# Output projection of layer 0: two early units loaded by GpSimd's queue, last column chunk split in all units

## The chip, the cores and the metric

The kernel runs on one core of one Trainium2 chip. The metric is the device time of one execution in microseconds (us), as the median of several runs. Before the change it is 2216.42 us (three runs, 2216.26 to 2216.97). "Faster" and "slower" are meant against that number.

Five engines matter here: TensorE (PE, matmuls; its weight loads are listed apart as PEld), VectorE (DVE), ScalarE (ACT), GpSimd (POOL) and SyncE (SP, which here only issues transfers). Each engine, and each queue of transfers, takes its instructions in a fixed order.

## What is computed

Two layers of a streaming encoder on 256 positions of width 2048, all in fp32. Cut to what the change touches, the reference is:

```python
for l in range(DEPTH):
    ...
    proj = h @ w_in[l]
    ...
    y_c = short_conv_mixer(sb, sc, sh, sconv_w[l])
    y_d = conformer_conv(ag, conf_w_dw[l], conf_b_dw[l], conf_ln_g[l], conf_ln_b[l])
    y = jnp.concatenate([y_a, y_b, y_c, y_d], axis=-1) @ w_out[l]
    x = layer_norm(ALPHA * x + (1.0 + gate_m) * y, post_mix_g[l], post_mix_b[l])
    h = layer_norm(x) * (1.0 + scale_f) + shift_f
    y = conv_ffn(h, ffn_w_up[l], ffn_w_conv[l], ffn_b_conv[l], ffn_w_down[l])
    ...
```

The change touches the product with `w_out` in layer 0: 2048 inputs (16 k tiles of 128, four each from the mixers a, b, c and d) by 2048 outputs, for two position tiles of 128.

## The kernel before

A weight tile goes through TensorE in one of two ways. **Exact**: the fp32 tile is used as it was loaded (tile name `wexact`), one fp32 matmul for each product; the profile counts such a matmul as two instructions. **Split**: the raw tile (`wraw`) is cast on ScalarE to a short format (`whi` or `thi`, L344), the rest is formed on VectorE by a subtraction (`wlo` or `tlo`, L345), the activation is split in the same way (`a`, L363 and L364), and three short-format matmuls stand for one product: high by high, high by low, low by high.

`out_proj` (L574) runs over three column chunks: columns 0 to 1023 in eight units of two k tiles, columns 1024 to 1535 in four units of four k tiles, and columns 1536 to 2047 in four units of four k tiles. I call them the first, second and last chunk. With `plain=(1024,)` in layer 0, the second chunk is exact, and so are the first `PLAIN_UNITS` = 2 units of the other two chunks; `exact` in `load_unit` (L703) says so. In layer 1 `plain` is empty, and all is split. The pairs `a` that were split once are kept for later chunks (`kept`).

The matmuls of the last chunk stand together at the end (`done`): position tile 0 through all four units, then position tile 1. After position tile 0, `finish` (L601) and `norm(0)` run on VectorE, then the normed rows are transposed on TensorE (`ps_xT`, L557), and the next product `first` (L501, the first columns of the feed-forward part) begins.

`weights` (L314) makes the tiles and issues their transfers. Exact tiles take buffers of the tags `whi` and `wlo` (four each) in turn, or "slot" buffers where `spare` is set (units 0 and 1 of the last chunk); raw tiles take one of four buffers, shared with the modulation weights `wmod` (1 MB each, multiplied and summed on VectorE at L193, the "mod step") and with the rows `gb` of the norm (L614). All these transfers stand in SP's queue, in the order in which the code makes them, so a transfer that waits for a buffer holds all that stand behind it. How many mod steps come between the units is set by `RATES`; a scheduler then orders each engine's instructions by its own estimates, and that order is fixed when the kernel is built. GpSimd does only small power operations and memsets.

## Time and profile before

| what | us |
|---|---|
| median of three runs | 2216.42 |
| the profiled execution, as timed | 2215.87 |
| its span, first to last instruction | 2214.1 |
| exact products of the first chunk, start on TensorE | 296.93 |
| second chunk, start on TensorE | 346.55 |
| last chunk, start on TensorE | 374.02 |
| transposes ahead of the feed-forward part, start | 402.03 |

The profile is one execution. Its times count from the first instruction; a row gives start, duration, engine, line, operation, output<-input and a count, and in brackets how long the engine had idled ahead of it and what ended that.

### The profile page before, as it was taken

The page shows a single profiled execution, that of the slowest core. Times are in us where ns is not written, and L with a number is a line of the kernel's source. Part 1 is how long each engine was busy: PE and PEld are TensorE (multiplying, and loading weights), DVE is VectorE, ACT ScalarE, POOL GpSimd, SP SyncE. Part 2 cuts the span into 40 slices and gives each one's busy share as a digit, 9 for nine tenths or more (in the row PEclk, how much of TensorE's full clock was granted, in tenths as well). Part 3 has the DMA queues.
Part 4 walks back from the last instruction along what each step waited for, and adds up shares of the span by engine and source line. Part 5 has one row for each costly group of instructions (what it writes and reads, how often), then busy time and mean ns, then how long its engine had stood idle before and what let it go on. Part 6 is the DMA issues. An engine that isn't in the chain of part 4 may idle for free. (4 is left out here: it accounts for less than half of the span.)

```text
span 2214.1 us, 28391 instructions
## 1 busy us (share of the span) xinstructions
PE 2182.7 (99%) x10868; PEld 1795.1 (81%) x10868; DVE 1705.3 (77%) x2269; ACT 1081.6 (49%) x1656; POOL 22.4 (1%) x38
## 2 busy tenths in 40 slices
PE   8999999999999999999999999999999999999997
PEld 6776865588888888888867988868888888888886
DVE  5657997798888888989958988877765656575776
ACT  3132731655454545545665555465444545464553
POOL 0000000000000000000000000000000000000000
PEclk9999999999999999999999999999999999999999
DMA  9999989598888889989757546856765555555553
GB/s 392 417 376 390 358 326 394 205 341 325 327 317 318 330 319 325 331 331 345 278 218 291 188 160 253 329 196 248 262 213 190 190 190 190 190 209 192 191 196 144
DMA packets 94442, 608.15 MB, mean 275 GB/s; under 512 B 10657, under 2 KB 10849, under 8 KB 28769
## 3 DMA queue, kind: packets, MB, share of 16 engines
q1 hardware_dynamic: 94178, 606.31, 74.3%
q8 instruction: 85, 1.39, 0.2%
q14 instruction: 51, 0.42, 0.0%
q10 hardware_dynamic: 128, 0.03, 0.0%
HBM read 604.17 MB, written 2.13 MB: 274 GB/s over the span
## 5 line engine op out<-in xcount | busy, mean ns | idle before, releaser
L344 ACT CAST whi<-wraw 128x1024 fp32r<-128x1024 f32 (+1 forms) x612 | 637.3, 1046 | 722.3 <-PE g_c L117 212.2
L345 DVE TENSOR_TENSOR wlo<-wraw,whi 128x1024 fp32r<-128x1024 f32 (+1 forms) x612 | 733.8, 1212 | 291.7 <-ACT whi L344 275.9
L193 DVE SCALAR_TENSOR_TENSOR wmod<-wmod,crep 128x2048 f32<-128x2048 f32 x192 | 438.1, 2286 | 71.7 <-DMA wmod<-in_w_mod_dram 70.8
L117 PE MATMUL v_c<-hT,whi 128*128 128x512 f32 x1408 | 489.2, 392 | 0.0
L117 PE MATMUL g_c<-hT,whi 128*128 128x512 f32 x1280 | 444.6, 392 | 0.0
L117 PE MATMUL v_c<-hT,wlo 128*128 128x256 f32 x1408 | 392.1, 279 | 0.0
L117 PE MATMUL d<-whi,a 128*128 128x512 f32 x1344 | 386.4, 389 | 0.0
L117 PE MATMUL g_c<-hT,wlo 128*128 128x256 f32 x1280 | 356.5, 278 | 0.0
L117 PEld LDWEIGHTS v_c<-hT,whi 128*128 128x128 f32 x1408 | 263.6, 187 | 59.3
L117 PEld LDWEIGHTS d<-whi,a 128*128 128x128 f32 x1344 | 252.0, 188 | 52.4
L117 PEld LDWEIGHTS g_c<-hT,whi 128*128 128x128 f32 x1280 | 239.7, 187 | 54.2
L117 PEld LDWEIGHTS v_c<-hT,wlo 128*128 128x128 f32 x1408 | 265.1, 188 | 0.1
L117 PEld LDWEIGHTS g_c<-hT,wlo 128*128 128x128 f32 x1280 | 241.0, 188 | 0.0
L117 PE MATMUL d<-wlo,a 128*128 128x512 f32 x672 | 232.9, 389 | 0.0
L117 PEld LDWEIGHTS d<-wlo,a 128*128 128x128 f32 x672 | 126.1, 188 | 26.2
L117 PE MATMUL o<-whi,a 128*128 128x512 f32 x352 | 102.1, 393 | 0.0
L363 ACT CAST a<-g 128x512 fp32r<-128x512 f32 x132 | 81.1, 615 | 17.0 <-PE d L117 15.7
L364 DVE TENSOR_TENSOR a<-g,a 128x512 fp32r<-128x512 f32 x132 | 88.7, 684 | 0.0
L501 PE MATMUL first<-wexact,hN 128*128 128x512 f32 x192 | 86.0, 598 | 1.2 <-ACT hN L120 1.0
L117 PEld LDWEIGHTS o<-whi,a 128*128 128x128 f32 x352 | 65.9, 188 | 14.9 <-issue 1.0
L1415 DVE SCALAR_TENSOR_TENSOR u<-g,par,u 128x254 f32<-128x254 f32 (+1 forms) x176 | 73.7, 476 | 0.0
L501 PEld LDWEIGHTS first<-wexact,hN 128*128 128x128 f32 x192 | 35.6, 192 | 41.2 <-issue 34.9
(311 smaller groups left out, 2161.9 us busy)
## 6 DMA issues: line engine op xcount, KB each, us to landing
wmod<-in_w_mod_dram SPq DMA_DIRECT2D x192, 1024.0 KB, 6.9
wraw<-in_ffn_w_up_dram SPq DMA_DIRECT2D x168, 1024.0 KB, 5.2
wraw<-in_ffn_w_down_dram SPq DMA_DIRECT2D x88, 1024.0 KB, 5.0
wexact<-in_w_in_dram SPq DMA_DIRECT2D x64, 512.0 KB, 11.4
wraw<-in_w_out_dram SPq DMA_DIRECT2D x24, 1024.0 KB, 5.8
wraw<-in_w_in_dram SPq DMA_DIRECT2D x24, 1024.0 KB, 5.2
wexact<-in_w_out_dram SPq DMA_DIRECT2D x16, 512.0 KB, 11.4
wexact<-in_ffn_w_up_dram SPq DMA_DIRECT2D x16, 512.0 KB, 5.7
```

The costliest lines, as they stand in the source:

```text
L117: pe.matmul(o, lhsT, rhs, start=start, stop=stop, skip_group_check=True)
L193: i = dve.scalar_tensor_tensor(out=raw, in0=raw, scalar=1.0, in1=crep, op0=ALU.mult, op1=ALU.mult, accum_out=col)
L344: held(act.copy(hi[:, :m], r), "cast")
L345: i = dve.tensor_tensor(out=lo[:, :m], in0=r, in1=hi[:, :m].bitcast(F32), op=ALU.subtract)
L363: act.copy(hi, src)
L364: dve.tensor_tensor(out=lo, in0=src, in1=hi.bitcast(F32), op=ALU.subtract)
L501: i = pe.matmul(ps, hN[kt // 4][:, kt % 4, t * P : (t + 1) * P], parts[kt], start=kt == 0, stop=kt == KT - 1, skip_group_check=True,)
L1415: dve.scalar_tensor_tensor(out=u[:, sh:], in0=x[:, : S - sh], scalar=col(k, j), in1=u[:, sh:], op0=ALU.mult, op1=ALU.add)
```

## The change

```diff
-    def weights(w, k0, nk, c0, width, exact=False, spare=0):
+    def weights(w, k0, nk, c0, width, exact=False, spare=0, queue=nc.sync):
...
-                nc.sync.dma_start(out=r[:, :m], in_=w.take(m, rows_of(l, k0 + k, per, c0, width)))
+                queue.dma_start(out=r[:, :m], in_=w.take(m, rows_of(l, k0 + k, per, c0, width)))
...
-                exact = c0 in plain or (bool(plain) and u < PLAIN_UNITS)
-                parts = weights(w, kt, nk, c0, width, exact, spare)
+                early = c0 == 0 and bool(plain) and u < PLAIN_UNITS
+                exact = c0 in plain or early
+                parts = weights(w, kt, nk, c0, width, exact, spare, nc.gpsimd if early else nc.sync)
```

It holds two edits. Units 0 and 1 of the first chunk stay exact, but their four transfers of 512 KB are issued by GpSimd. Units 0 and 1 of the last chunk are split now: four exact tiles become two raw tiles, four casts and four subtractions, and the k tiles 0 to 3, exact in the first chunk, need their activation pairs (`a<-ya`) split as well. Nothing changes in layer 1, nor in any engine's order behind layer 0's `first` products.

Three places show how the order moves. **SP's queue** at the start of the output projection; each row is a transfer, `x2` two alike. Before:

```order
L328 DMA wexact<-in_w_in_dram 128x1024 x2
L192 DMA wmod<-in_w_mod_dram 128x2048 x5
L328 DMA wexact<-in_w_out_dram 128x1024 x2
L192 DMA wmod<-in_w_mod_dram 128x2048
L328 DMA wexact<-in_w_out_dram 128x1024 x2
L192 DMA wmod<-in_w_mod_dram 128x2048
L333 DMA wraw<-in_w_out_dram 128x2048
```

And with the change, in SP's queue:

```order
L328 DMA wexact<-in_w_in_dram 128x1024 x2
L192 DMA wmod<-in_w_mod_dram 128x2048 x7
L333 DMA wraw<-in_w_out_dram 128x2048
L192 DMA wmod<-in_w_mod_dram 128x2048
L333 DMA wraw<-in_w_out_dram 128x2048
```

The four `wexact<-in_w_out_dram` are gone from it. They stand on GpSimd instead, behind the memsets of the attention part and ahead of the power operation of mixer d's norm:

```order
L1064 MEMSET rope 64x256
L1065 MEMSET rope 64x256
L328 DMA wexact<-in_w_out_dram 128x1024 x4
L147 TENSOR_TENSOR rd<-rd,mhalf 128x2
```

**VectorE in the first chunk**: `convD` and `rd`, `dgD` belong to mixer d's norm, each `wlo` row is one split unit (2 to 7, in order), and the rows begin behind the last product of `yc`. Before:

```order
L874 SCALAR_TENSOR_TENSOR convD<-ps_mean,convD 128x256 x4
L193 SCALAR_TENSOR_TENSOR wmod,sums_4_1598<-wmod,crep 128x2048
L364 TENSOR_TENSOR a<-yc,a 128x2x256 x2
L193 SCALAR_TENSOR_TENSOR wmod,sums_4_1598<-wmod,crep 128x2048
L345 TENSOR_TENSOR wlo<-wraw,whi 128x1024 x2
...
L364 TENSOR_TENSOR a<-yd,a 128x2x256
L345 TENSOR_TENSOR wlo<-wraw,whi 128x1024 x2
L193 SCALAR_TENSOR_TENSOR wmod,sums_4_1598<-wmod,crep 128x2048
L364 TENSOR_TENSOR a<-yd,a 128x2x256
L345 TENSOR_TENSOR wlo<-wraw,whi 128x1024 x2
L193 SCALAR_TENSOR_TENSOR wmod,sums_4_1598<-wmod,crep 128x2048
L345 TENSOR_TENSOR wlo<-wraw,whi 128x1024 x2
```

With the change:

```order
L193 SCALAR_TENSOR_TENSOR wmod,sums_4_1598<-wmod,crep 128x2048 x2
L875 SCALAR_TENSOR_TENSOR convD<-ps_mean,convD 128x256 x4
L345 TENSOR_TENSOR wlo<-wraw,whi 128x1024 x2
L193 SCALAR_TENSOR_TENSOR wmod,sums_4_1598<-wmod,crep 128x2048
L894 TENSOR_SCALAR rd<-ps_var 128x2
L364 TENSOR_TENSOR a<-yc,a 128x2x256
L900 TENSOR_SCALAR dgD<-cst,rd 128x128 x2
L364 TENSOR_TENSOR a<-yc,a 128x2x256
...
L364 TENSOR_TENSOR a<-yd,a 128x2x256
L364 TENSOR_TENSOR a<-ya,a 128x2x256 x2
L345 TENSOR_TENSOR wlo<-wraw,whi 128x1024 x2
L193 SCALAR_TENSOR_TENSOR wmod,sums_4_1598<-wmod,crep 128x2048
L345 TENSOR_TENSOR wlo<-wraw,whi 128x1024 x2
```

The splits `a<-yc` go behind unit 2's subtractions, one of them between `rd` and `dgD`; the two new splits `a<-ya` stand ahead of unit 6's subtractions. The number of mod steps between the units is the same.

**VectorE around the end of the second chunk**: `o_102400` and `o_102410` are the second chunk's results for position tiles 0 and 1, `o_153600` the last chunk's for tile 0. Before:

```order
L604 TENSOR_TENSOR yg<-o_102400_1969,gate_2_1368 128x512
L605 SCALAR_TENSOR_TENSOR x_96<-x_96,yg 128x512
L193 SCALAR_TENSOR_TENSOR wmod,sums_4_1598<-wmod,crep 128x2048
L608 BN_STATS st_o_1602<-x_96 128x6
L604 TENSOR_TENSOR yg<-o_102410_1970,gate_2_1368 128x512
L193 SCALAR_TENSOR_TENSOR wmod,sums_4_1598<-wmod,crep 128x2048
L605 SCALAR_TENSOR_TENSOR x_97<-x_97,yg 128x512
L223 TENSOR_TENSOR mod_4_2026<-sums_4_1598,par 128x16
L608 BN_STATS st_o_1603<-x_97 128x6
L345 TENSOR_TENSOR wlo<-wraw,whi 128x1024 x4
L604 TENSOR_TENSOR yg<-o_153600_2052,gate_2_1368 128x512
```

With the change, the same stretch:

```order
L193 SCALAR_TENSOR_TENSOR wmod,sums_4_1598<-wmod,crep 128x2048
L605 SCALAR_TENSOR_TENSOR x_97<-x_97,yg 128x512
L223 TENSOR_TENSOR mod_4_2026<-sums_4_1598,par 128x16
L608 BN_STATS st_o_1603<-x_97 128x6
L345 TENSOR_TENSOR tlo<-wraw,thi 128x1024 x4
L345 TENSOR_TENSOR wlo<-wraw,whi 128x1024 x4
L604 TENSOR_TENSOR yg<-o_153600_2070,gate_2_1368 128x512
```

The four new subtractions `tlo` (units 0 and 1) stand behind the second chunk's last statistics and ahead of units 2 and 3. On TensorE, position tile 0 of the last chunk is 48 short-format matmuls now, and three of position tile 1 stand among them, one ahead of the first `tlo` product and two near the end; 45 of position tile 1 follow.

## The prediction

> **What bounds the kernel now.** I read the page's busy times first, then the stretches around the change, the waits of TensorE, the last link of the chain of waits, and the timelines of TensorE, VectorE, ScalarE and SyncE between 260 and 440 us.

> ```profile
> span 2214.1 us, 28391 instructions
> PE 2182.7 (99%) x10868; PEld 1795.1 (81%) x10868; DVE 1705.3 (77%) x2269; ACT 1081.6 (49%) x1656; POOL 22.4 (1%) x38
> ...
> 436.00:960.00 524.00, 524.00 (x2947) 455.37 (x2948) 462.35 (x565) 272.38 (x383) 0.00 (x0) 1.00 0.89 326
> 295.00:335.00 40.00, 38.00 (x144) 25.58 (x145) 38.50 (x53) 16.79 (x22) 0.70 (x1) 1.00 0.99 377
> ...
> PE ps_xT L557 <- ACT xn L120: 3.7, 3, 3.1
> PE o L117 <- DMA wexact<-in_w_out_dram: 2.9, 1, 2.9
> ...
> 1962.76 239.42 PE d L117 x1056
> ```

> TensorE is busy for 99% of the span, and from 436 to 960 us for 524.00 of 524. What layer 0's output projection gains or loses before 436 therefore reaches the end undiminished. Two waits stand inside the changed stretch: 2.9 us for the exact weights and 3.1 us for the normed rows. But from 295 to 335 us VectorE is busy for 38.50 of 40 (third figure after the comma), as closely as TensorE's 38.00. A short-format matmul takes 239.42 / 1056 = 0.2267 us.

> **First edit: the four loads on GpSimd.** The rows are TensorE's, SyncE's and VectorE's timelines, and one line of the exact tile's answer.

> ```profile
> 268.13 7.07 PE L117 MATMUL C_c<-hF,wexact 128*128 128x256 f32 x32
> 296.93 14.00 PE L117 MATMUL o<-wexact,ya 128*128 128x512 f32 x32 [2.88 <-DMA wexact<-in_w_out_dram]
> 346.55 7.03 PE L117 MATMUL o<-wexact,ya 128*128 128x512 f32 x16
> ...
> 290.94 0.86 SPq L328 DMA_DIRECT2D wexact<-in_w_out_dram  x2
> ...
> 308.43 1.28 DVE L364 TENSOR_TENSOR a<-yc,a 128x512 fp32r<-128x512 f32 x2
> 311.85 2.35 DVE L345 TENSOR_TENSOR wlo<-wraw,whi 128x1024 fp32r<-128x1024 f32 x2
> 317.36 0.48 DVE L899 TENSOR_SCALAR dgD<-cst,rd 128x128 f32<-128x128 f32 x2 [0.88 <-POOL rd L147]
> 339.95 2.36 DVE L345 TENSOR_TENSOR wlo<-wraw,whi 128x1024 fp32r<-128x1024 f32 x2 [0.95 <-ACT whi L344]
> ```

> SyncE issues the first two loads at 290.94, behind modulation weights, and TensorE starts on them at 296.93 after 2.88 us idle. On GpSimd's queue they wait only for buffers that the C group's products (from 268.13 on) give back, about 268 us for the first and 275 for the second by the products' order. So the 2.88 us go, and the exact products start near 294.05 (296.93 - 2.88).

> That gain stops at the next stage. The order in VectorE's queue has the same subtractions and mod steps. Unit 2's first `wlo` ends at 311.85 + 1.18 = 313.02; with the two `a<-yc` (1.28 less overlap, 1.21 net) behind it, at 311.8. From there on, one `a<-yc` fills the 0.88 gap ahead of `dgD`, the two new `a<-ya` add about 1.2, and the 0.95 gap ahead of unit 7 takes some back: unit 6 comes about 0.6 later than before, unit 7 about 0.4 earlier. TensorE, busy 38.00 of 40 with 1.93 of its idle time (up to 296.93) ahead of the first product, has no slack to make up for a late unit, and a unit that isn't ready can't start early. The chunk's end at 346.55 moves by -0.4 to +0.6; I take **0**. Should VectorE not bind, the bound on this side is -2.9.

> The operation that no row shows is a large load on GpSimd's queue. From below it costs nothing (the loads land 20 us ahead of need). [...]

> ```profile
> 287.59 0.69 DVE L364 TENSOR_TENSOR a<-yb,a 128x512 fp32r<-128x512 f32 x1 [0.89 <-ACT a L363]
> ...
> DMA to landing us min/median/max: 2.9/9.5/14.9
> ```

> [...] I take **0**, nearest to the median landing of 9.5 after 275, and keep +4.7. [...]

> The second chunk stays exact and keeps its 27.47 us (346.55 to 374.02).

> **Second edit: the tail.** First the rows of TensorE, then VectorE, with layer 1's, where all is split, among them; then the loads; then one group each of subtractions and casts.

> ```profile
> 374.02 3.60 PE L117 MATMUL o<-wexact,ya 128*128 128x512 f32 x8
> 402.03 1.97 PE L557 MATMUL ps_xT<-cst,xn 128*128 128x128 f32 x8 [3.14 <-ACT xn L120]
> 435.42 0.47 PE L117 MATMUL v_c<-hT,whi 128*128 128x512 f32 x1
> 1463.66 1.36 PE L557 MATMUL ps_xT<-cst,xn 128*128 128x128 f32 x8 [0.24 <-ACT xn L120]
> 1495.80 0.48 PE L117 MATMUL v_c<-hT,whi 128*128 128x512 f32 x1
> ...
> 372.12 2.29 DVE L193 SCALAR_TENSOR_TENSOR wmod<-wmod,crep 128x2048 f32<-128x2048 f32 x1
> 375.53 2.28 DVE L193 SCALAR_TENSOR_TENSOR wmod<-wmod,crep 128x2048 f32<-128x2048 f32 x1
> 378.45 0.69 DVE L608 BATCH_NORM_STATS2 st_o<-x 128x6 f32<-128x512 f32 x1
> 390.96 0.69 DVE L604 TENSOR_TENSOR yg<-o,gate 128x512 f32<-128x512 f32 x1 [5.95 <-PE o L117]
> 391.57 0.15 DVE L629 TENSOR_REDUCE offs_o<-offs_o 128x1 f32<-128x4 f32 x1
> 1452.58 0.69 DVE L604 TENSOR_TENSOR yg<-o,gate 128x512 f32<-128x512 f32 x1 [4.30 <-PE o L117]
> ...
> 363.72 2.29 DVE L193 SCALAR_TENSOR_TENSOR wmod<-wmod,crep 128x2048 f32<-128x2048 f32 x1 [0.19 <-DMA wmod<-in_w_mod_dram]
> 365.04 1.60 SPq L333 DMA_DIRECT2D wraw<-in_w_out_dram  x2
> 377.84 0.33 SPq L614 DMA_DIRECT2D gb<-in_post_mix_b_dram  x1
> ...
> 378.92 1.99 ACT L344 CAST whi<-wraw 128x1024 fp32r<-128x1024 f32 x2 [38.05 <-DMA wraw<-in_w_out_dram]
> 386.52 0.63 ACT L622 ACTIVATE junk<-gb 128x512 f32<-128x512 f32 x1 [2.96 <-DMA gb<-in_post_mix_b_dram]
> ...
> L345 DVE TENSOR_TENSOR tlo<-wraw,thi 128x1024 fp32r<-128x1024 f32 x12 | 14.2, 1219 | 0.0
> L344 ACT CAST thi<-wraw 128x1024 fp32r<-128x1024 f32 x12 | 12.1, 1050 | 3.4 <-DMA wraw<-in_ffn_w_down_dram 1.8 <-DMA wraw<-in_w_out_dram 1.6
> ```

> Now the exact products of the tail start at once, at 374.02; position tile 0 ends with `yg` at 390.96, and the transposes follow 402.03 - 390.96 = 11.07 later. That chain stays (layer 1: 1463.66 - 1452.58 = 11.08). TensorE idles 3.14 ahead of it, because too little of position tile 1 was left.

> With the change, position tile 0's 8 exact products (7.03 for 16 instructions at 346.55) become 24 short matmuls (5.4), so TensorE has less to do; but VectorE now stands ahead of it. In its order the first `tlo` comes behind the second chunk's last statistics: 378.45 + 0.69, about 379.1. It takes 1.22, so the first low products start at 380.3. Meanwhile the two raw tiles take the buffers of earlier mod steps (the later one, at 363.72, is through at 366.0), land by 375.5 (the median of 9.5), and their casts (1.05 each) are done by 377.6: earlier than VectorE. What was started at 374.02 now waits about 5 us on VectorE. Then 49 matmuls (48, and one of position tile 1 among them) x 0.2267 = 11.1 end at 391.4, and the transposes come at 402.5: **+0.5**. Position tile 1's 45 matmuls (10.2) fill until 401.6, so TensorE idles 0.9 there instead of 3.14.

> That idle time has a price after it. From the transposes to `v_c` layer 0 takes 435.42 - 402.03 = 33.39, layer 1, with 0.24 idle ahead, 1495.80 - 1463.66 = 32.14.

> ```profile
> 296.00:298.00 2.00, 1.07 (x3) 0.59 (x4) 2.00 (x5) 0.00 (x0) 0.00 (x0) 1.00 1.07 442
> 402.00:403.00 1.00, 0.97 (x5) 0.97 (x6) 0.00 (x0) 0.68 (x1) 0.00 (x0) 0.50 0.93 393
> 405.00:406.00 1.00, 1.00 (x3) 0.43 (x3) 0.93 (x4) 1.00 (x5) 0.03 (x1) 0.99 0.00 0
> ```

> The granted clock (third from the right) is 0.50 at 402 and back at 0.99 at 405; after the 2.88 us ahead of 296.93 it stayed 1.00. With 0.9 idle I take layer 1's time: 32.14 - 33.39 = **-1.25**. But the wait at 375 to 380 is longer than 3.14, so the low clock should show there: some 3 us at half rate (402 to 405) are 1.5 us of matmuls lost, **+1.5**; its bounds are 0 and 1.8. [...]

> `gb` is pushed behind the raw tiles: it takes the buffers that the `tlo` subtractions free, until about 383.9, against 377.84 now. It landed 8.7 later (386.52); that would be 392.6, and with the four `junk` steps (2.5) behind it 395.1. VectorE's `offs_o`, which needs them, stands right behind `yg` (391.57, then 392.0): at worst +3.1. I take 0, since two transfers fewer stand ahead of it, so that it may land some 4 us sooner. The 4 casts lie in ScalarE's 38.05 idle, and cost nothing.

> Sum: 0 + 0.5 - 1.25 + 1.5 = **+0.75**. The profiled execution was timed at 0.55 under the median; I put the difference on the median: 2216.42 + 0.75 = **2217.2**.

> **Rivals.** *A: both gains arrive.* VectorE doesn't bind in either place, and the exact products' 2.88 goes through. The tail starts at 371.14, takes 11.1 + 11.07, and 32.14 to `v_c`: 425.45 instead of 435.42, -9.97, **2206.5**. Against it: VectorE's 38.50 of 40. *B: only the tail's gain.* The `tlo` would be ready at 374.02: 374.02 + 22.17 + 32.14 = 428.33, -7.1, **2209.3**. For it: layer 1's tail runs like that. Against it: the two mod steps at 372.12 and 375.53 and the statistics at 378.45 stand ahead in VectorE's fixed order. *C: slower.* The last raw tile is issued only when the mod step at 375.53 gives its buffer back, at 377.84 (now 365.04 and just behind). It decides from a landing of 8.5 on: its first `wlo` is due at 380.3 + 36 x 0.2267 = 388.5, and a cast and a subtraction (1.0 and 1.18) earlier is 386.3. With 14.9 it lands at 392.7, its `wlo` is there at 394.9, 6.4 late: +7.2, **2223.6**. For it: the raw tiles of now took 378.92 - 365.04 = 13.9. Against it: two transfers of 1 MB fewer stand ahead. *D: GpSimd's loads late*, +4.7: 0.75 + 4.7, **2221.9**. That the first edit brings no load earlier at all changes the sum by nothing.

> **How the numbers follow.** My forecast has 0.78, A 0.03, B 0.08, C 0.07, D 0.04. The forecast's own bounds are -2.9 (first edit) and -1.5 (clock) below, and +0.6 (unit 6), +0.3 (clock) and +3.1 (`gb`) above: from 2212.8 to 2221.2. The unknown price of GpSimd's loads takes the upper end to D, 2221.9, which is my range. A measurement of this kernel can tell about 0.2%, 4.4 us, from no change: faster (A, B) 0.11, same 0.78, slower (C, D) 0.11.

> **What would show it.** Right: no wait of `o` for `wexact`, but one of about 2 us for `wlo` before the same 346.5; then a wait of about 5 us on `tlo` from 375 on, with a granted clock of 0.50 behind it; the transposes near 402.5 to 404 with under 1.5 idle, and `v_c` about 32.1 after them. Wrong: a first chunk that ends 2 us or more earlier (VectorE didn't bind), `tlo` ready before 377, a wait for `wraw` in the last two units, or exact products that start after 297.

## The result, and the profile after

The changed kernel takes 2220.38 us as the median of 12 runs (2217.82 to 2227.84), the kernel before 2216.55 of 12 (2214.31 to 2218.11): a ratio of 1.002, 95% interval 1.0011 to 1.0029, so 2.4 to 6.4 us slower. A second set gave 2219.92 against 2216.64, ratio 1.0016 (1.0007 to 1.0025). The median lies inside the predicted range, and the change is smaller than the 4.4 us (0.2%) that the forecast took as no change. But it is 3.2 us above the predicted 2217.2, and where the forecast said +0.75 it is +3.3 to +3.8.

The profiled execution of the changed kernel was timed at 2217.82, the fastest of its 12. Its page and its waits of TensorE:

```profile
span 2216.0 us, 28439 instructions
PE 2182.0 (98%) x10884; PEld 1800.8 (81%) x10884; DVE 1710.6 (77%) x2275; ACT 1086.1 (49%) x1662; POOL 25.0 (1%) x42
...
PE o L117 <- DVE tlo L345: 5.7, 1, 5.7
...
PE ps_var L117 <- ACT sqD L881: 2.3, 1, 2.3
...
PE ps_xT L557 <- ACT xn L120: 1.5, 3, 1.0
```

The wait for `wexact` is gone, and the 3.1 us ahead of the transposes are 1.0. In their place stand 5.7 us for `tlo`, which was forecast, and 2.3 us for `sqD`, the squares of mixer d's norm, which was not. TensorE's timeline has these places in order:

```profile
292.19 7.03 PE L117 MATMUL o<-wexact,ya 128*128 128x512 f32 x16
...
310.80 0.61 PE L117 MATMUL ps_var<-ones,sqD 128*128 128x1 f32 x4 [2.29 <-ACT sqD L881]
...
311.94 0.73 PE L117 MATMUL o<-wlo,a 128*128 128x512 f32 x2 [0.19 <-DVE wlo L345]
...
347.23 7.03 PE L117 MATMUL o<-wexact,ya 128*128 128x512 f32 x16
...
381.00 0.79 PE L117 MATMUL o<-tlo,a 128*128 128x512 f32 x1 [5.69 <-DVE tlo L345]
...
405.56 1.36 PE L557 MATMUL ps_xT<-cst,xn 128*128 128x128 f32 x8 [0.98 <-ACT xn L120]
...
437.69 0.48 PE L117 MATMUL v_c<-hT,whi 128*128 128x512 f32 x1
```

The exact products start at 292.19, directly behind the C group, where before the mean's products began (292.17). Yet the second chunk starts at 347.23 instead of 346.55. `v_c` comes 437.69 - 435.42 = 2.27 later, and the rest of the span is as long as before (1778.31 us behind it, 1778.68 before). So all of the loss lies in this stretch. The granted clock, third from the right, shows where (stretches of the changed kernel):

```profile
310.00:314.00 4.00, 3.00 (x20) 2.61 (x20) 4.00 (x6) 3.88 (x5) 0.00 (x0) 0.95 0.97 403
314.00:318.00 4.00, 4.00 (x13) 3.20 (x14) 3.38 (x8) 1.39 (x2) 1.03 (x1) 0.63 0.94 354
...
378.00:379.00 1.00, 0.00 (x0) 0.00 (x0) 1.00 (x3) 0.00 (x0) 0.00 (x0) 0.71 1.00 426
381.00:385.00 4.00, 4.00 (x9) 3.13 (x10) 4.00 (x4) 2.67 (x4) 0.00 (x0) 0.50 0.89 328
385.00:386.00 1.00, 1.00 (x5) 0.87 (x4) 1.00 (x2) 0.46 (x1) 0.00 (x0) 0.88 1.00 393
```

There are two stretches of low clock: one behind the wait for `sqD` (busy time times what the clock lacks: 4.00 x 0.37 and 3.00 x 0.05, an estimated 1.6 us lost; four `whi` products took 2.05 us from 313.96 on, at 0.50, and 1.07 from 317.73 on, at 1.00), and one that begins in the wait for `tlo` and outlasts it (4.00 x 0.50 and 0.12, 2.1 us lost). VectorE's timeline says why TensorE waited in both places; `sqD` itself is a row of ScalarE:

```profile
304.92 2.28 DVE L193 SCALAR_TENSOR_TENSOR wmod<-wmod,crep 128x2048 f32<-128x2048 f32 x1
...
307.13 2.28 DVE L193 SCALAR_TENSOR_TENSOR wmod<-wmod,crep 128x2048 f32<-128x2048 f32 x1
...
309.34 1.41 DVE L875 SCALAR_TENSOR_TENSOR convD<-ps_mean,convD 128x256 f32<-128x256 f32 x4
...
310.12 0.63 ACT L881 ACTIVATE sqD<-convD 128x512 f32<-128x512 f32 x1 [3.48 <-DVE convD L875]
...
310.68 2.35 DVE L345 TENSOR_TENSOR wlo<-wraw,whi 128x1024 fp32r<-128x1024 f32 x2
...
379.13 0.69 DVE L608 BATCH_NORM_STATS2 st_o<-x 128x6 f32<-128x512 f32 x1
379.74 4.61 DVE L345 TENSOR_TENSOR tlo<-wraw,thi 128x1024 fp32r<-128x1024 f32 x4
...
394.49 0.69 DVE L604 TENSOR_TENSOR yg<-o,gate 128x512 f32<-128x512 f32 x1 [5.59 <-PE o L117]
```

In the profile of before `convD` ran at 304.90:

```profile
304.90 1.41 DVE L874 SCALAR_TENSOR_TENSOR convD<-ps_mean,convD 128x256 f32<-128x256 f32 x4
```

The new order puts two mod steps ahead of it, so it runs at 309.34, and the squares that ScalarE makes from it come 4.4 us later. The first `tlo` stands behind the second chunk's last statistics, as forecast.

GpSimd's loads were early. Its timeline and one row of the page's DMA part:

```profile
266.48 0.71 POOL L328 DMA_DIRECT2D wexact<-in_w_out_dram  x1 [60.98 <-PE C_c L117]
...
275.53 0.54 POOL L328 DMA_DIRECT2D wexact<-in_w_out_dram  x1 [0.64 <-PE C_c L117]
...
wexact<-in_w_out_dram POOLq DMA_DIRECT2D x4, 512.0 KB, 8.4
```

The last was issued at 275.53. By the median of 8.4 us to landing it was there near 284, some 8 us before the first use, and TensorE shows no wait for any of the four.

### The profile page after: what moved, and what is told of

Its sections match the earlier page's. It is cut to its first block, busy times and chain, and to the rows that moved or that the text cites. A ratio compares the mean times of both kernels' runs of the same rounds, so it can differ in the third digit from the quotient of the medians.

```text
span 2216.0 us, 28439 instructions
## 1 busy us (share of the span) xinstructions
PE 2182.0 (98%) x10884; PEld 1800.8 (81%) x10884; DVE 1710.6 (77%) x2275; ACT 1086.1 (49%) x1662; POOL 25.0 (1%) x42
## 5 line engine op out<-in xcount | busy, mean ns | idle before, releaser
L344 ACT CAST whi<-wraw 128x1024 fp32r<-128x1024 f32 (+1 forms) x612 | 637.1, 1046 | 678.8 <-PE g_c L117 210.5
L345 DVE TENSOR_TENSOR wlo<-wraw,whi 128x1024 fp32r<-128x1024 f32 (+1 forms) x612 | 733.6, 1213 | 283.6 <-ACT whi L344 268.6
L193 DVE SCALAR_TENSOR_TENSOR wmod<-wmod,crep 128x2048 f32<-128x2048 f32 x192 | 438.1, 2286 | 78.9 <-DMA wmod<-in_w_mod_dram 78.0
L117 PE MATMUL v_c<-hT,whi 128*128 128x512 f32 x1408 | 489.2, 392 | 0.0
L117 PE MATMUL g_c<-hT,whi 128*128 128x512 f32 x1280 | 444.6, 392 | 0.0
L117 PE MATMUL v_c<-hT,wlo 128*128 128x256 f32 x1408 | 392.1, 279 | 0.0
L117 PE MATMUL d<-whi,a 128*128 128x512 f32 x1344 | 386.4, 389 | 0.0
L117 PE MATMUL g_c<-hT,wlo 128*128 128x256 f32 x1280 | 356.5, 278 | 0.0
L117 PEld LDWEIGHTS v_c<-hT,whi 128*128 128x128 f32 x1408 | 263.6, 187 | 59.1
L117 PEld LDWEIGHTS d<-whi,a 128*128 128x128 f32 x1344 | 252.0, 188 | 52.4
L117 PEld LDWEIGHTS g_c<-hT,whi 128*128 128x128 f32 x1280 | 239.7, 187 | 54.1
L117 PEld LDWEIGHTS v_c<-hT,wlo 128*128 128x128 f32 x1408 | 265.3, 188 | 0.1
L117 PEld LDWEIGHTS g_c<-hT,wlo 128*128 128x128 f32 x1280 | 241.1, 188 | 0.0
L117 PE MATMUL d<-wlo,a 128*128 128x512 f32 x672 | 232.9, 389 | 0.0
L117 PEld LDWEIGHTS d<-wlo,a 128*128 128x128 f32 x672 | 126.1, 188 | 26.2
L117 PE MATMUL o<-whi,a 128*128 128x512 f32 x352 | 102.9, 395 | 0.0
L363 ACT CAST a<-g 128x512 fp32r<-128x512 f32 x132 | 81.1, 615 | 17.1 <-PE d L117 15.7
L364 DVE TENSOR_TENSOR a<-g,a 128x512 fp32r<-128x512 f32 x132 | 88.8, 685 | 0.0
L117 PEld LDWEIGHTS o<-whi,a 128*128 128x128 f32 x352 | 66.8, 190 | 14.2 <-issue 0.5
```

What stands on the lines that cost most here:

```text
L117: pe.matmul(o, lhsT, rhs, start=start, stop=stop, skip_group_check=True)
L193: i = dve.scalar_tensor_tensor(out=raw, in0=raw, scalar=1.0, in1=crep, op0=ALU.mult, op1=ALU.mult, accum_out=col)
L344: held(act.copy(hi[:, :m], r), "cast")
L345: i = dve.tensor_tensor(out=lo[:, :m], in0=r, in1=hi[:, :m].bitcast(F32), op=ALU.subtract)
L363: act.copy(hi, src)
L364: dve.tensor_tensor(out=lo, in0=src, in1=hi.bitcast(F32), op=ALU.subtract)
```

## The experiments

Two spans are read in every run. The first chunk is counted from the first row of TensorE behind the C group (an exact product, or `ps_mean` where that comes first) to the start of the second chunk; the rest from there to the first `v_c`. Both are from one profiled execution of each kernel. My theory after the result: TensorE's new waits, and a low clock behind each, cost what the edits save. The rivals were GpSimd's loads, later waits, and, for the first chunk, VectorE's sheer amount of work. All medians are of 11 or 12 runs (of before 12 to 35); a ratio is to the kernel before on the same chip, and is not simply that of the two medians. The runs stem from several chips, on which the medians of before lie within 0.3 us of each other. Low clock means the microseconds of matmul work that it cost, added up as above over the whole stretch.

| kernel | median us | ratio (95%) | first chunk | rest | low clock |
|---|---|---|---|---|---|
| before | 2216.4 to 2216.6 | | 54.38 | 88.87 | 1.5 |
| changed | 2220.38 | 1.0020 (1.0011, 1.0029) | 55.04 | 90.46 | 3.8 |
| `again` | 2219.92 | 1.0016 (1.0007, 1.0025) | 56.64 | 90.57 | 5.6 |
| `edit1` | 2217.51 | 1.0001 (0.9993, 1.0010) | 56.64 | 89.05 | 5.1 |
| `edit2` | 2217.68 | 1.0009 (1.0000, 1.0018) | 54.88 | 90.10 | 1.7 |
| `mods_first` | 2215.02 | 0.9992 (0.9983, 1.0001) | 56.65 | 85.68 | 3.4 |
| `conv_first` | 2217.46 | 1.0002 (0.9994, 1.0011) | 54.60 | 90.56 | 2.2 |
| `edit1_conv` | 2215.70 | 0.9994 (0.9986, 1.0003) | 54.11 | 90.14 | 4.5 |
| `keep_warm` | 2217.68 | 1.0011 (1.0003, 1.0020) | 56.65 | 88.63 | 3.4 |
| `fewer_mods` | 2215.75 | 0.9998 (0.9989, 1.0006) | 50.43 | 93.19 | 3.6 |
| `both_tlo` | 2212.73 | 0.9985 (0.9976, 0.9994) | 54.61 | 87.61 | 1.7 |
| `edit2_tlo` | 2212.80 | 0.9985 (0.9977, 0.9994) | 55.10 | 85.35 | 1.7 |
| `best075` | 2213.10 | 0.9985 (0.9976, 0.9995) | 53.02 | 87.53 | 0.0 |
| `best05` | 2212.49 | 0.9984 (0.9975, 0.9992) | 50.38 | 90.36 | 2.8 |

**The changed kernel again**, without an edit.

> The changed kernel once more, for a second profile and a second set of times. Theory 1 (the loss lies in the two stretches of low clock and in the wait on tlo): the first chunk ends at 347.2 and v_c begins near 437.7 as in the first profile, within 1 us, and the median is 2220 again; if this execution is above 2219, the extra stands between 310 and 320 or between 375 and 390. Theory 2 (GpSimd's loads are late in some executions): the extra stands ahead of 297, as a wait of o on wexact. Theory 3 (later waits): v_c begins at 437.7 and the extra comes after 440.

The first profile had caught a short low clock. In this one, of the same program, the same wait has a longer one behind it (timeline and stretches of `again`):

```profile
309.82 0.61 PE L117 MATMUL ps_var<-ones,sqD 128*128 128x1 f32 x4 [2.31 <-ACT sqD L881]
...
347.83 7.03 PE L117 MATMUL o<-wexact,ya 128*128 128x512 f32 x16
...
310.00:314.00 4.00, 3.82 (x18) 3.31 (x18) 4.00 (x3) 3.98 (x5) 0.00 (x0) 0.62 0.99 338
314.00:318.00 4.00, 4.00 (x12) 3.29 (x13) 3.07 (x8) 0.41 (x1) 1.03 (x1) 0.53 0.99 391
```

The program ran 1.0 us earlier here up to this wait (exact products from 291.19), and started the second chunk 0.6 later: the chunk took 56.64 instead of 55.04, and 3.3 us of work went to the low clock instead of 1.6. Four kernels with this order (`again`, `edit1`, `mods_first`, `keep_warm`) took 56.64 or 56.65, so 2.3 us longer than before is the usual case, and the first profile's 0.7 the mild one. This is where part of the distance between that profile and the median comes from. Neither profile shows a wait for `wexact`, and nothing is lost behind `v_c`. Both are of executions below the median, so they do not say what the longest (up to 2227.84) lost.

**Each edit alone.** The first keeps `exact = c0 in plain or (bool(plain) and u < PLAIN_UNITS)` and only takes the queue; the second keeps `exact = c0 in plain or early` and leaves the queue at SyncE.

> Only the first edit: units 0 and 1 of the first chunk loaded by GpSimd's queue, last chunk as before. Theory 1: the exact products start at 292.2, TensorE idles 2.3 on mixer d's squares instead of 2.9 on the weights and may see a low clock behind it, the chunk ends between 345.5 and 346.5, and the tail is that of before; 2215.5 to 2217, with a scatter of about 4 us as before. Theory 2 (GpSimd's loads bring the loss and the scatter): about 2219, single runs up to 2228.

> Only the second edit: all units of the last chunk split, early loads on SyncE. Theory 1 (the loss is the tail's): the wait of 2.9 on wexact stands, the chunk ends at 346.5 to 347.5, TensorE waits 5 to 6 us on tlo, v_c begins near 437; 2218 to 2220 and the wide scatter. Theory 2 (the loss is the first edit's): 2216 to 2217.5 with a scatter of 4 us.

A row of TensorE from each, `edit1` first:

```profile
311.05 0.61 PE L117 MATMUL ps_var<-ones,sqD 128*128 128x1 f32 x4 [1.81 <-ACT sqD L881]
...
380.48 0.79 PE L117 MATMUL o<-tlo,a 128*128 128x512 f32 x1 [5.46 <-DVE tlo L345]
```

The first edit by itself costs 0.9 us in the median, with an interval around nothing, and 2.3 in the first chunk of its profile, whose end came later (349.07) than the expected 345.5 to 346.5; the median lies half a microsecond above its expected range. Its order also has two mod steps ahead of `convD`; the profile shows 1.81 us of waiting for `sqD` and the same low clock. None of its 11 runs was above 2220.25, so nothing here puts the runs up to 2228 down to GpSimd's loads. The second edit costs 1.0 in the median; its ratio says 2.0, with 0 to 4.0. Its profile has the 2.9 us on `wexact` still, 5.46 on `tlo`, and `v_c` at 436.80. It missed its 2218 in the median, though five of its 11 runs lay above 2217.7. The times alone don't part the two edits, since the second's interval reaches the whole loss. The profiles do: 2.3 us of the first chunk go with the first edit, 1.2 us of the rest (90.10 against 88.87) with the second. So each carries a part.

**Mod steps ahead of the second chunk's results.** One dependence that only orders:

```diff
-            dve.tensor_tensor(out=y, in0=p, in1=box["gate"][:, cols], op=ALU.mult)
+            i = dve.tensor_tensor(out=y, in0=p, in1=box["gate"][:, cols], op=ALU.mult)
+            if plain and q == 2:
+                tc.add_manual_dep(i.ins, last_step[0], order_dep, reason="mod steps first")
```

It lets VectorE do the last two mod steps in the 5.8 us that it had idled ahead of 371.46; two `tlo` then come ahead of the statistics.

> The changed kernel, but VectorE does the two mod steps of the second chunk's end ahead of that chunk's results instead of between them; SyncE's order is the same. Theory 1 (tlo waits for VectorE): first tlo at 378 instead of 381, TensorE idles under 3 us there, the low clock behind it goes or shrinks, v_c 2.9 to 4.9 earlier, 2215.5 to 2217.5. Rival (tlo waits for the raw tiles' landing): first tlo stays at 381 and the time at 2220.

```profile
348.42 7.03 PE L117 MATMUL o<-wexact,ya 128*128 128x512 f32 x16
...
376.77 0.73 PE L117 MATMUL o<-thi,a 128*128 128x512 f32 x2 [0.71 <-ACT thi L344]
...
379.24 0.50 PE L117 MATMUL o<-tlo,a 128*128 128x512 f32 x1 [1.74 <-DVE tlo L345]
...
401.97 1.36 PE L557 MATMUL ps_xT<-cst,xn 128*128 128x128 f32 x8 [0.84 <-ACT xn L120]
```

In this timeline of `mods_first` the wait for `tlo` is 1.74 us instead of 5.69, no low clock follows it, and the rest falls from 90.5 to 85.68, although the first chunk took its full 56.65. On VectorE the mod steps fill the gap only in part, since the first of them waits 2.74 us for its load and starts at 370.69; the first `tlo` starts at 377.96 instead of 379.74. The median is 4.9 below `again`, a little under the expected range. The raw tiles cost 0.71 us at most; `tlo` had waited for its place in VectorE's line.

**Work in the wait.** The changed kernel with 22 products whose result nothing uses, behind the first `thi` product:

```diff
+                if plain and u == 0 and k == 0 and t == 0 and n == 1:
+                    junk = ms_tile("warm")
+                    for _ in range(22):
+                        pe.matmul(junk, ah, hi[:, cols[0]], start=True, stop=True, skip_group_check=True)
```

> The changed kernel with 22 more products, whose result nothing uses, on TensorE behind the last chunk's first high product, 5.0 us of work in its wait for tlo. Theory 1 (a low clock behind the wait costs some 2 us beside it): the first tlo product stays where it is (381 to 381.6), the clock stays at 1.00 behind it, and the transposes follow 22.2 to 22.8 after it instead of 24.6; 2217.5 to 2218.5. Rival (the slow stretch behind the wait is VectorE or the transfers): still 24.6, 2220.

```profile
376.69 5.17 PE L598 MATMUL warm<-thi,a 128*128 128x512 f32 x22
...
382.61 0.50 PE L117 MATMUL o<-tlo,a 128*128 128x512 f32 x1 [0.74 <-DVE tlo L345]
...
405.32 1.36 PE L557 MATMUL ps_xT<-cst,xn 128*128 128x128 f32 x8 [0.88 <-ACT xn L120]
...
381.00:385.00 4.00, 3.25 (x14) 2.36 (x13) 4.00 (x5) 2.00 (x2) 0.00 (x0) 1.00 0.95 297
...
393.93 0.16 DVE L633 TENSOR_REDUCE offs_o<-offs_o 128x1 f32<-128x4 f32 x1 [3.42 <-ACT junk L626]
```

Here the first `tlo` product started at 382.61, later than expected only because the first chunk ended at 348.83 (33.78 behind it, as in `again`). The clock stays at 1.00, and from the first `tlo` product to the transposes it is 405.32 - 382.61 = 22.71 instead of 24.56 and 24.65. So about 1.9 us of the tail go with the low clock. Two smaller things differ as well, and nearly cancel: two products of position tile 1 (0.45 us) no longer stand among tile 0's, and `yg` starts at 394.25 behind `offs_o` (last row), 0.58 later than tile 0's last product allows. With them the low clock comes to about 2.0, near the 2.1 added up from the rows. The median of 2217.68 is 2.2 below `again`; the intervals of the two ratios overlap, so the stretch shows this better than the time.

**`convD` first.** The two latest mod steps (`steps` lists them as they are made) get an order behind it:

```diff
+                if l == 0:
+                    for m in steps[-2:]:
+                        tc.add_manual_dep(m, i.ins.name, order_dep, reason="the mean comes first")
```

> The changed kernel, with VectorE's convD of mixer d's norm ahead of the two mod steps instead of behind them. Theory 1 (convD behind two mod steps makes TensorE wait 2.3 us for the squares, and the low clock behind that wait takes the rest of what the early loads gave): the wait for sqD goes, at most 2 us of waiting for wlo are left, no clock of 0.50 between 310 and 320, first chunk 53 to 54 us from its first exact product to the second chunk instead of 55.0 to 56.6; 2216 to 2218. Rival (VectorE's order sets the chunk's end, whatever TensorE does ahead): the second chunk starts at 347 to 348 as now, 2220.

> The first edit alone, with convD ahead of the two mod steps. Theory 1: 2 to 3.5 us faster than the first edit alone (2217.5), so 2214 to 2215.5: the 2.9 us of waiting for the weights then mostly arrive. Rival: 2217.5 as without.

```profile
312.14 0.74 PE L117 MATMUL o<-wlo,a 128*128 128x512 f32 x2 [1.42 <-DVE wlo L348]
317.25 0.70 PE L117 MATMUL ps_rD<-dgD,ones 128*128 128x256 f32 x2 [0.27 <-DVE dgD L908]
324.24 1.20 PE L117 MATMUL o<-whi,a 128*128 128x512 f32 x4 [0.41 <-ACT whi L347]
...
336.87 0.73 PE L117 MATMUL o<-wlo,a 128*128 128x512 f32 x2 [0.19 <-DVE wlo L348]
346.98 7.03 PE L117 MATMUL o<-wexact,ya 128*128 128x512 f32 x16
```

The wait for `sqD` and the low clock behind it are gone in `conv_first`, and the time falls by 2.5 us. But TensorE now waits four times, 1.42 + 0.27 + 0.41 + 0.19 = 2.29, mostly on VectorE, and the chunk takes 54.60, not the expected 53: no less than before the change. `edit1_conv` came out 1.8 below `edit1`, at 2215.70, a little short of its 2214 to 2215.5. The 1.42 us left did bring a low clock in `edit1_conv` (311 to 315 us, 1.6 us lost), none in `conv_first`. So theory 1 holds for the wait on `sqD`, and the rival for the chunk's end: the early start is not worth 2.9 us even where the clock stays up. A later run bears this out: `both_tlo`, with the same order here, lost 1.7 us to a low clock in the first chunk and took 54.61, as long as `conv_first` without one.

**VectorE's work in the first chunk.** `conv_first` with other rates of the mod steps, which moves four of them out of the first chunk; the splits `a<-ya` follow them:

```diff
-    dict(B=1.3, attend=1.3, C=1.9, out=1.0, out_next=1.55, out_last=0.0, up=0.7, down=0.7, down_next=0.7, down_last=0.0),
+    dict(B=1.3, attend=1.3, C=1.9, out=0.5, out_next=2.55, out_last=0.0, up=0.7, down=0.7, down_next=0.7, down_last=0.0),
```

> As conv_first, with the modulation weights' rate halved in the first chunk (0.5 a unit instead of 1.0) and raised in the second (2.55 instead of 1.55); four mod steps, 9 us of VectorE, leave the first chunk, and the two splits a<-ya follow them. Theory 1 (VectorE's work sets the first chunk's end, and eats what the early loads give): the waits of 2.3 us in the chunk go, it takes 52 to 52.6 us from its first exact product instead of 54.6, without low clock. Rival (TensorE's own work or the transfers set it): 54.6 as in conv_first. The tail may get worse, since more mod steps stand ahead of tlo: 2213 to 2218.

The stretch from 295 to 335 us and TensorE's timeline of `fewer_mods`:

```profile
295.00:335.00 40.00, 40.00 (x164) 29.31 (x163) 37.91 (x53) 19.83 (x25) 1.03 (x1) 1.00 0.84 309
...
342.27 4.02 PE L117 MATMUL o<-wexact,ya 128*128 128x512 f32 x9
...
374.34 1.22 PE L117 MATMUL o<-thi,a 128*128 128x512 f32 x2 [4.44 <-ACT thi L347]
...
377.74 0.79 PE L117 MATMUL o<-tlo,a 128*128 128x512 f32 x1 [2.18 <-DVE tlo L348]
```

TensorE is busy for 40.00 of 40, the chunk takes 50.43, 4.2 less than in `conv_first` and 4 less than before the change; even more than the forecast 52. Of the 4.2, 2.29 are the four waits; the other 1.9 stand in no bracket, though TensorE's rows of the chunk hold 202 instructions in both. So VectorE's work had set the chunk's end. Whether the early loads pay once that work is lighter is likely, since no wait for `wexact` is left, but not shown: no run has the lighter chunk with the loads on SyncE. But the moved steps come back in the tail: the raw tiles, whose transfers stand behind theirs, are late by 4.44 us and `tlo` by 2.18, the rest takes 93.19, and 2215.75 is no clear gain on the kernel before.

**Putting the orders together.** `both_tlo` is the changed kernel with `convD` first, the mod steps first, and two `tlo` ahead of the additions to `x`; `edit2_tlo` has the last two orders on the second edit alone; `best075` and `best05` are `both_tlo` with two or four mod steps moved to the second chunk. The new one among these orders, where `i` is now the addition to `x` behind each `yg` of the second chunk, and `tail_subs` lists the `tlo`:

```diff
+            if plain and q == 2:
+                tc.add_manual_dep(i.ins, tail_subs[1], order_dep, reason="the last chunk comes first")
```

> The changed kernel with three orders on VectorE: convD ahead of its two mod steps, the last two mod steps ahead of the second chunk's results, and the first two tlo ahead of the additions to x. Theory 1: the gains add up, first chunk 53 to 54, TensorE waits under 2 us on tlo, no low clock in either place; 2210.5 to 2213. Rival (one wait takes the other's place, the transfers land late): 2214 to 2215, as with the mod steps alone (2215.0).

> The second edit alone (early loads on SyncE), with the last two mod steps ahead of the second chunk's results and two tlo ahead of the additions to x, as in both_tlo. Theory 1 (all of both_tlo's gain is the tail's, the first edit gives nothing while VectorE sets the first chunk's end): 2212 to 2214, as both_tlo (2212.7). Rival (the early loads are worth their 2.9 us once nothing else is late): 2215 to 2216.

> both_tlo with two mod steps moved from the first chunk to the second, where VectorE waits 5.8 us. Theory 1: first chunk at most 1 us shorter (its first wait for wlo stands ahead of the moved steps), tail as in both_tlo; 2211 to 2213. Rival (the moved steps' transfers hold tlo up): 2214 to 2216.

> both_tlo with four mod steps moved from the first chunk to the second. Theory 1: first chunk 2 us shorter, tail as in both_tlo; 2209.5 to 2212. Rival (the moved steps' transfers hold tlo up): 2214 to 2216.

All four lie between 2212.49 and 2213.10, 3.3 to 3.9 us below the kernel before, with intervals under 1. (One of `both_tlo`'s 11 executions took 7995 us; nothing here explains it, and it moves no median.) They can't be told apart. `best075` and `best05` missed their ranges by 0.1 and 0.5 us. That `edit2_tlo` equals `both_tlo` says that on this version the first edit gives nothing that these times, with intervals of 2 us on either side, can show. The chain moves each time: in `best05` the first chunk takes 50.38, but TensorE waits 4.70 us for `thi`; in `both_tlo` it waits 3.29 ahead of the transposes, because the rows `gb` land late (`junk` begins at 388.37 and `offs_o` waits for it until 390.97). `edit2_tlo` is the simplest of them (timeline, waits for `tlo` and transposes):

```profile
375.83 0.50 PE L117 MATMUL o<-tlo,a 128*128 128x512 f32 x1 [1.14 <-DVE tlo L348]
379.31 0.50 PE L117 MATMUL o<-tlo,a 128*128 128x512 f32 x1 [0.42 <-DVE tlo L348]
399.51 1.36 PE L563 MATMUL ps_xT<-cst,xn 128*128 128x128 f32 x8 [0.99 <-ACT xn L120]
```

## Why the prediction was right, and where it was off

- **The first chunk's end ("I take 0").** The mechanism named, VectorE's amount of work, is what `fewer_mods` showed: 4.2 us less of chunk for four mod steps less. Where `convD` was not pushed back, the chunk came out as forecast: +0.5 in `edit2`, +0.2 in `conv_first`. The step that failed is the reading of VectorE's order there. The prediction followed `a<-yc` and `a<-ya` and let TensorE wait for `wlo`. The rows of the change also showed two mod steps moved ahead of `convD`, and `convD` feeds `sqD`, which TensorE waits for ahead of `wlo`. The wait has the size that was given (2.3 and 0.2, against "about 2"), but the low clock behind it was not counted. The term measured +0.7 in the first profile and +2.3 in four others, against 0 and bounds of -0.4 to +0.6. The exact products' start was misread too, without effect: 292.19 against 294.05, since the mean's products no longer stand ahead of them.
- **The tail's start.** Forecast for the first low product: 380.3, with the chunk's end where it was. Measured 381.00 with that end 0.7 later: right to 0.1.
- **The low clock behind it (+1.5, bounds 0 and 1.8).** A low clock came there as forecast, but the size was small, and no run shows the bound of 1.8: 2.1 in the first profile, and about 2.0 by `keep_warm`, with work in the wait. The low clock lasted from 378.42 to 385.24 us, twice the 3.41 us of before (401.61 to 405.03).
- **The transposes (+0.5) and what follows (-1.25).** From the second chunk's start to the transposes 58.33 instead of 55.48, +2.85: 0.5 and the 2.1 of low clock, and 0.25 that the forecast left out at the last product of position tile 0. That product starts at 393.99 and its row lasts 0.39, where 0.2267 was counted, and `yg` starts another 0.11 later, at 394.49. From the transposes to `v_c` 437.69 - 405.56 = 32.13, where 32.14 was forecast.
- **`gb`.** Taken as 0 and so it was: `junk` began at 390.44 and `offs_o` ran in its place at 395.10. That it is next in line shows in `keep_warm` and `both_tlo`.
- **Rivals.** A fell with the first chunk. B describes what an order can get: with `tlo` at 375.83 (`edit2_tlo`) `v_c` begins at 431.64, against B's 428.33 for 374.02. C and D fell: the last raw tile's cast began at 383.46, ahead of 386.3, and GpSimd's loads were early. The change was slower by another way: waits that the order makes, each with its low clock.
- **The range.** That the median lies in it is luck in part. Without the allowances for `gb` (+3.1) and for GpSimd's loads (+4.7), neither of which cost anything, the forecast's own bounds end at 2217.2 + 0.6 + 0.3 = 2218.1, below both medians. No run shows the +4.7: in all eleven profiles with these loads on GpSimd TensorE has no wait for `wexact` in the first chunk, and in the first of them the last load was issued at 275.53. Of the signs named, the wait for `wlo` came as one for `sqD`, and the transposes at 405.56 instead of 402.5 to 404.
- **The sum.** The terms as measured give 2.3 + 1.6 to 1.7 (rest 90.46 and 90.57 against 88.87), +3.9 to +4.0, and the medians +3.8 and +3.3. In single profiles the two edits add up to this as well (2.4 and 1.7); in medians they give 0.9 and 1.0 (by the ratios 0.2 and 2.0), with intervals of 2 us on either side. That difference stays open.

## What to carry to other kernels

Where an engine waits, read what its next instructions need in the other engine's new order row by row, not only those that the change is about: a step of background work that slips ahead of a small operation delays it by its full length (4.4 us for two here, 2.3 of them a wait of TensorE). The earlier loads gave nothing that these times show where VectorE's work set the chunk's end (2212.73 with them in `both_tlo`, 2212.80 without them in `edit2_tlo`); measure such a limit by taking work off the other engine before moving transfers. And price every wait of TensorE with the low clock that can follow it, 1.5 to 3.4 us here, which may be more than the wait itself; where waits on another engine took that time anyway, it cost nothing more here (first chunk 54.61 in `both_tlo` with 1.7 us lost in it, 54.60 in `conv_first` with none).

## What the runs showed of the hardware

The length of a wait did not decide by itself here whether the clock fell. Behind 1.8 to 2.3 us of waiting for `sqD`, with one-column products behind it, it fell in all five profiles with that wait, and cost 1.6 us of work once and 3.3 to 3.4 elsewhere; behind 1.42 to 1.43 us of waiting for `wlo` it fell in two profiles (`edit1_conv`, `both_tlo`) and stayed up in two (`conv_first`, `best075`). Behind 2.88 and 2.92 us ahead of the exact weights it did not fall (before, `edit2`), behind 2.75 at the same place it did (`edit2_tlo`), and only 1.4 us after the work had resumed at 295.82 (at 297.18, read in steps of 0.1 us):

```profile
297.00:300.00 3.00, 3.00 (x5) 1.21 (x4) 3.00 (x6) 0.00 (x0) 0.00 (x0) 0.53 0.98 407
```

Behind 3.29 us ahead of the transposes it stayed at 1.00 (`both_tlo`), behind 3.14 it fell (before).

```profile
292.38:295.80 3.42, 1.68 (x8) 1.14 (x6) 3.42 (x5) 1.71 (x4) 0.00 (x0) 1.00 0.97 405
...
293.77:297.18 3.41, 1.35 (x3) 0.68 (x4) 3.41 (x5) 0.36 (x1) 0.00 (x0) 1.00 1.04 430
```

That the same program lost 1.6 us in one execution and 3.3 in another agrees with this: behind the wait for `sqD` the first profile had one such window of low clock (313.56 to 316.98), `again` two (310.96 to 317.80).
